# Loading and normalising the tokens of a decoder step: a diagonal matrix of the norm's factors in the transposing matmul, sample tokens first, and the first weight pair by feature blocks

## The chip, the cores and the metric

The kernel runs on one core of one Trainium2 chip. The core has a matrix engine (TensorE, PE in the profile; PEld is its loading of the stationary operand), three engines for elementwise work (VectorE = DVE, ScalarE = ACT, GpSimd = POOL) and SyncE (SP), from whose queue this kernel issues all its transfers. The metric is the time of one execution in microseconds, the median of several runs.

## The reference

One step of a one-layer decoder over 1,024 prompt tokens and 8 x 4 sample tokens, all in float32, model width 1,024, feed-forward width 2,816:

```python
def rmsnorm(x, g):
    y = xf * lax.rsqrt(jnp.mean(xf * xf, axis=-1, keepdims=True) + RMS_EPS)
    return (y * g.astype(jnp.float32)).astype(x.dtype)

def swiglu(x, w_gate, w_up, w_down):
    return (jax.nn.silu(x @ w_gate) * (x @ w_up)) @ w_down

# trunk_layer
x = half_ffn(x, 0, 0, 1)             # x + 0.5 * rmsnorm(swiglu(rmsnorm(x, g0), ...), g1)
h = rmsnorm(x, g[2])                 # then one input projection, mLSTM heads and
...                                  # sliding-window attention heads
x = x + rmsnorm(u @ w_out[l], g[3])  # one output projection
x = half_ffn(x, 1, 4, 5)
```

The outputs are the new tokens and the new states and caches. For the sample sequences the new key and value caches are the last 124 of the 128 old rows followed by the 4 new ones.

## The kernel before

**Layout.** The tokens are cut into four quarters q = 0..3. A quarter holds 256 prompt tokens and 8 sample tokens, so that its moving operand has 264 columns (`QW`). Features lie on the 128 partitions, in 8 blocks k = 0..7, kept in four tiles kp = 0..3 of two blocks each. Since tokens come from memory with a token on each partition, they are transposed on TensorE when they are loaded.

**Precision.** Each float32 operand of a large product is split into a high part (`Xh`, `wh`, a cast on ACT, L196) and the rest (`Xl`, `wl`, a subtraction on DVE, L197). A product is then three matmuls: high by high, high by low, low by high (`mm3` and the loops in `ffn`, all issued in `pe`, L154; transposes are issued there at L151).

**Loading (`load_tokens`, `token_norm`, `load_x`, L296 to L369).** For each quarter four transfers bring 128 x 512 pieces of the prompt (L298); for q = 0 two more bring the sample tokens after them. ACT and DVE sum the squares (L314, L317), and `rstd` makes the factor 1/root in ten small DVE instructions (L265 to L276), two of which make the first guess from the bits of the number. Meanwhile TensorE transposes the raw tokens in 16 transposes into four PSUM banks (`xT`, L151), ACT copies each bank out (`xr`, L353), POOL copies the sample columns in (L356). The factors are put on a row by six PE instructions (`rb`) and copied to `rrow` (L283). The raw tokens are stored in a scratch for the residual (`stash`, L290). `blocks` (L380) then multiplies each half tile by gain and row on DVE (`xb`, L385) and splits it (`Xh`, `Xl`). `sums` (L393) makes differences of these blocks, which the fast matrix products of the later weight pairs use.

**The feed-forward part (`ffn`, L694).** The 22 column blocks of the gate and up matrices are taken in 11 pairs. Pair p = 0 is multiplied plainly (`NPLAIN` = 1, tiles `pl`): for each quarter, each matrix and each column block m, the eight feature blocks are summed in one PSUM bank, 8 x 3 matmuls; 384 in all. From p = 1 on, a scheme with seven products in place of eight is used (tiles `gu`), on sums and differences made by `sums`. Then comes the down product (`pd`). Weights arrive as 512 KB transfers in two `raw` buffers (`plain_units`, `gu_units`, L634 and L670) and are split as units, four units ahead (`AHEAD` = 3).

**Order.** `Order` runs generators beside the matmul loops: each `yield` gives a delay in estimated PE time, `tick` runs what is due after each product, `need` runs tasks until a key is there, `take` hands out the next split weights. `XW` and `XQ` are the delays of loading. The framework then schedules the instructions of each engine in its own order from an estimate of when they are ready, within the data's dependencies; `high_priority` blocks go ahead. Each engine runs its list in order. After the program's start `load_x(0)` runs until the second tile is split, then weights are filled, then the other quarters are spawned (`program`, L1760).

**Later.** `post` (L428) ends each product that goes back to the residual: it loads the stored tokens (`x`, from `xs`), computes the norm of the product, adds, and stores. `swa_sample` (L1190) handles the sample's attention; it copies the 124 old cache rows from memory to memory with two transfers (L1195), and loads the old caches again as tiles `kc` and `vc`. `Last.finish` holds the end of the kernel: a `rstd`, then the last output tiles.

## Time and profile before

| what | value |
| --- | --- |
| median of 3 runs | 2020.64 us (2015.86 to 2020.72) |
| the profiled execution's own time | 2019.21 us |
| its span, first to last instruction | 2017.4 us |
| mean granted TensorE clock | 0.996 |
| PE busy | 1986.5 us, 16,178 matmul instructions |
| DVE busy | 1168.4 us |
| ACT busy | 874.9 us |
| POOL busy | 35.6 us |
| bytes moved, mean rate | 216.66 MB, 107 GB/s |

The span begins with the first instruction and ends with the last; the execution's own time is 1.81 us longer. Times in the views are microseconds from the span's start. A busy PE is not a PE at its best pace: matmuls overlap, so what counts is the distance from the start of one to the start of the next. A row of the timeline gives the start, the time from the first start to the last end, the engine, the line, the operation, the tiles (out<-in), the shapes, the number of instructions merged, and in brackets the idle time before it with what ended it. A row of a stage table gives the stretch, its length and the busy time of each engine with the number of instructions.

### The profile page before, as it was taken

To read this page: it belongs to the slowest core of one execution; us is meant where nothing else is said; L and a number is where in the kernel's file an instruction comes from. 1 tells how busy PE (TensorE), PEld (TensorE's weight loads), DVE (VectorE), ACT (ScalarE), POOL (GpSimd) and SP (SyncE) were. 2 spreads that over 40 slices of the span, in tenths; PEclk is the share of its full clock that TensorE was granted. 3 is DMA by queue.
4 is the path that set the end of the run, shared out by engine and by line. 5 is a ranking of instruction groups with operands and counts; after the bars stand their busy time and mean duration, and the time that the engine had idled before them with its cause. 6 is when DMAs were issued, how large, how long until landed. Compare 5 with 4: busy or idle time off the path is not lost.

```text
span 2017.4 us, 40347 instructions
## 1 busy us (share of the span) xinstructions
PE 1986.5 (98%) x16178; PEld 1942.6 (96%) x16178; DVE 1168.4 (58%) x2822; ACT 874.9 (43%) x2087; POOL 35.6 (2%) x166
## 2 busy tenths in 40 slices
PE   7999999999999999999999999999999999999997
PEld 7999999999999999987999999999999999999997
DVE  5855555557238436467556758785555556534764
ACT  6533333336336332346244655353333334533553
POOL 0000000000000001100101000000000000000000
PEclk9999999999999999999999999999999999999999
DMA  6122222226346343201214143322222223545773
GB/s 234 65 85 77 90 69 74 76 95 177 108 142 208 104 102 124 68 1 38 68 53 134 57 133 116 108 78 82 65 84 80 91 64 120 167 129 162 226 223 116
DMA packets 279690, 216.66 MB, mean 107 GB/s; under 512 B 21032, under 2 KB 252640, under 8 KB 279488
## 3 DMA queue, kind: packets, MB, share of 16 engines
q1 hardware_dynamic: 279504, 214.11, 35.0%
q8 instruction: 126, 2.06, 0.5%
q14 instruction: 60, 0.49, 0.1%
HBM read 172.39 MB, written 42.49 MB: 107 GB/s over the span
## 4 chain that ended last, share of the span: by engine, by line
PE 91%; DVE 3%; DMA 3%; ACT 2%; issue 1%; SPq 0%; DVEq 0%; ACTq 0%
PE gu L154 41%; PE pd L154 23%; PE pz L154 7%; PE pw L154 4%; PE pl L154 4%; PE pv L154 3%; PE po L154 2%; DMA raw<-ffn_w_down 2%; PE cs L154 1%; PE rb L154 1%; PE swo L154 1%; PE sws L154 1%; PE E L154 1%; ACT wh L196 1%; PE swp L151 1%
## 5 line engine op out<-in xcount | busy, mean ns | idle before, releaser
L154 PE MATMUL gu<-Xh,wh 128*128 128x264 f32 x2240 | 636.6, 284 | 0.0
L154 PE MATMUL gu<-Xl,wh 128*128 128x264 f32 x2240 | 636.0, 284 | 0.0
L154 PE MATMUL gu<-Xh,wl 128*128 128x264 f32 x2240 | 635.1, 284 | 0.0
L197 DVE TENSOR_TENSOR wl<-raw,wh 128x512 fp32r<-128x512 f32 x458 | 301.6, 670 | 384.3 <-ACT wh L196 376.5
L154 PE MATMUL pd<-hq,wh 128*128 128x264 f32 x2816 | 520.8, 286 | 0.1
L196 ACT CAST wh<-raw 128x512 fp32r<-128x512 f32 x458 | 270.1, 602 | 459.4 <-PE pd L154 193.2
L154 PEld LDWEIGHTS pd<-hq,wh 128*128 128x128 f32 x2816 | 437.8, 189 | 0.4 <-ACT yo L853 0.4
L154 PEld LDWEIGHTS gu<-Xh,wh 128*128 128x128 f32 x2240 | 421.1, 188 | 0.5 <-ACT sc L752 0.2
L154 PEld LDWEIGHTS gu<-Xh,wl 128*128 128x128 f32 x2240 | 421.6, 188 | 0.0
L154 PEld LDWEIGHTS gu<-Xl,wh 128*128 128x128 f32 x2240 | 421.3, 188 | 0.0
L154 PE MATMUL pd<-hq,wl 128*128 128x264 f32 x1408 | 401.1, 285 | 0.0
L154 PEld LDWEIGHTS pd<-hq,wl 128*128 128x128 f32 x1408 | 265.4, 188 | 0.2 <-DVE wl L197 0.2
L752 ACT COPY sc<-gu 128x264 f32<-128x264 f32 x240 | 91.0, 380 | 272.2 <-PE gu L154 268.0
L197 DVE TENSOR_TENSOR wl<-ws,wh 128x512 fp32r<-128x512 f32 x160 | 108.8, 690 | 87.6 <-ACT wh L196 84.7
L763 DVE TENSOR_TENSOR h<-gu,sc 128x264 f32<-128x264 f32 x120 | 51.8, 432 | 102.2 <-PE gu L154 83.3
L154 PE MATMUL pz<-xh,wh 128*128 128x264 f32 x352 | 102.3, 291 | 0.6 <-DVE z L1684 0.6
L154 PE MATMUL pz<-xh,wl 128*128 128x264 f32 x352 | 100.8, 286 | 0.0
L154 PE MATMUL pz<-xl,wh 128*128 128x264 f32 x352 | 100.5, 285 | 0.0
L196 ACT CAST wh<-ws 128x512 fp32r<-128x512 f32 x160 | 95.9, 623 | 4.1 <-PE pl L154 2.5
L764 ACT ACTIVATE h<-h 128x264 f32<-128x264 f32 x120 | 50.9, 425 | 106.5 <-DVE h L763 106.5
L769 DVE TENSOR_TENSOR sc<-gu,sc 128x264 f32<-128x264 f32 x120 | 51.6, 432 | 56.8 <-PE gu L154 51.4
L154 PE MATMUL pl<-Xh,wh 128*128 128x264 f32 x256 | 72.9, 299 | 3.3 <-ACT Xh L196 2.1
(368 smaller groups left out, 2969.6 us busy)
## 6 DMA issues: line engine op xcount, KB each, us to landing
raw<-ffn_w_down SPq DMA_DIRECT2D x80, 512.0 KB
raw<-ffn_w_gate SPq DMA_DIRECT2D x44, 512.0 KB
raw<-ffn_w_up SPq DMA_DIRECT2D x44, 512.0 KB
h<-h SPq DMA_DIRECT2D x80, 264.0 KB
hq<-h SPq DMA_DIRECT2D x160, 132.0 KB
raw<-ffn_w_down SPq DMA_DIRECT2D x40, 384.0 KB
x<-xs SPq DMA_DIRECT2D x48, 264.0 KB
raw<-w_in SPq DMA_DIRECT2D x21, 512.0 KB
```

The costliest lines, as they stand in the source:

```text
L151: K.nc.tensor.transpose(out, lhsT, rhs)
L154: K.nc.tensor.matmul(out, lhsT, rhs, start=start, stop=stop, **kw)
L196: K.nc.scalar.copy(hi, src)
L197: (eng or K.nc.vector).tensor_tensor(lo, src, hi.bitcast(F32), op=ALU.subtract)
L752: nc.scalar.copy(sc[n][:, g], ps)
L763: nc.vector.tensor_tensor(d, bk[tg, g], sc[n][:, g], op=ALU.add)
L764: nc.scalar.activation(d, d, AF.Silu)
L769: nc.vector.tensor_tensor(sc[n][:, g], src, sc[n][:, g], op=ALU.add)
```

## The change

The loading and the first pair are rewritten; smaller edits follow from that.

- Transfers: sample tokens first, then the four pieces of quarter 0, then the weights of pair 0 as eight 256 KB pieces, one for two feature blocks of one matrix (`first_loads`), then quarter 1 into the two `raw` buffers. The tables for the Silu function are asked for at the start (`warm`).
- The norm comes before the transposing: `token_norm` gives the factor r and its inverse. A diagonal matrix of r (`diagonal`, one DVE instruction for 128 tokens) is the moving operand of an ordinary float32 matmul (L154's form) in place of the identity in a transpose, so that the bank holds normalised tokens, transposed.
- Out of the bank ACT writes the high part with the gain as scale (two halves), DVE writes the low part in one instruction for each half, and ACT copies the normalised tokens to `xn`. `blocks` is no longer used there. POOL copies the sample columns into three tiles in place of one.
- The scratch for the residual now holds normalised tokens, and `post` of phase 1 multiplies them by the inverse factor (one DVE instruction for each of 16 tiles). `sums` of phase 0 has to multiply by the gain itself (for each pair of quarters 8 half tiles on DVE and 8 on ACT).
- `first_pair` multiplies quarter 0 feature tile by feature tile into four banks at a time; quarters 1 to 3 go column block by column block as before.
- `rstd` makes its first guess in one instruction in place of two, everywhere in the kernel.
- The memory-to-memory copies of the caches are gone; four transfers from `kc` and `vc` write those rows.

```diff
-XW = [2.0, 0.15, 0.2]
+XW = [2.0, 0.15, 4.0]
-XQ = [0, 0.0, 4.0, 10.0]
+XQ = [0, 3.0, 10.0, 20.0]
-SUMS = {(2, 0, 0): 0, (3, 0, 0): 1}
+SUMS = {1: {(1, 1, 1): 0, (3, 0, 0): 1}, 3: {(2, 0, 0): 0, (3, 0, 0): 1}}
...
+    K.C, K.vs = [K.cp.tile([P, 4, 129], F32, tag=x, name=x) for x in ("C", "vs")]
...
+def gain_rows(K):
...
+    return graw
+def load_gains(K, graw):
...
+def rstd(K, ss, scale=1.0 / D, eps=EPS, root=False):
     nc.vector.tensor_scalar(v, ss, scale, eps, op0=ALU.mult, op1=ALU.add)
-    ri = r.bitcast(I32)
-    nc.vector.tensor_scalar(ri, v.bitcast(I32), 1, None, op0=ALU.arith_shift_right)
-    nc.vector.tensor_scalar(ri, ri, -1.0, float(0x5F3759DF), op0=ALU.mult, op1=ALU.add)
+    nc.vector.tensor_scalar(r.bitcast(I32), v.bitcast(I32), -0.5, float(0x5F3759DF), op0=ALU.mult, op1=ALU.add)
     nc.vector.tensor_tensor(t, r, v, op=ALU.mult)
     nc.vector.tensor_tensor(t, t, r, op=ALU.mult)
...
     nc.vector.scalar_tensor_tensor(t, r, -0.5 * 0.375 ** 3, v, op0=ALU.mult, op1=ALU.mult)
     nc.vector.tensor_tensor(t, t, r, op=ALU.mult)
     nc.vector.scalar_tensor_tensor(r, t, 1.5 * 0.375, r, op0=ALU.add, op1=ALU.mult)
...
+    nc.vector.tensor_tensor(u, v, r, op=ALU.mult)
+    return r, u
...
+def load_tokens(K, q):
+    if q == 1:
+        t = [raw_tile(K, [2, 512]) for _ in range(2)]
+        K.t[q] = [[x[:, i] for i in range(2)] for x in t]
+    else:
+        K.t[q] = [[slot(K, "xt")[:, 0:512] for _ in range(2)] for _ in range(2)]
     for i in range(2):
...
+        for j in range(2):
+            K.nc.sync.dma_start(K.t[q][j][i],
+                                K.A["x_prompt"][0, (2 * q + j) * P:(2 * q + j + 1) * P, i * 512:(i + 1) * 512])
+def first_loads(K):
+    A, nc = K.A, K.nc
+    K.t, K.w0 = {}, {}
+    K.xt = [slot(K, "xt")[0:32, 0:512] for _ in range(2)]
+    for i in range(2):
+        nc.sync.dma_start(K.xt[i], A["x_sample"].rearrange("b t d -> (b t) d")[:, i * 512:(i + 1) * 512])
+    load_tokens(K, 0)
+    for kp in range(4):
+        for mat, n in enumerate(("ffn_w_gate", "ffn_w_up")):
+            K.w0[kp, mat] = slot(K, "w0")[:, 0:512].rearrange("p (k m) -> p k m", k=2)
+            nc.sync.dma_start(K.w0[kp, mat], A[n][0, 0].rearrange("(k p) m -> p k m", p=P)[:, 2 * kp:2 * kp + 2, 0:256])
+    load_tokens(K, 1)
 def token_norm(K, tt, both=False):
...
-    for j, t in enumerate(tt):
+    for j, t in reversed([*enumerate(tt)]):
         for i in range(2):
             o = ss[0:w, n * i + j:n * i + j + 1]
-            if both and i == 0:
+            if both and (w < P or (j == 0 and i)):
                 nc.vector.tensor_tensor_reduce(out=jk, in0=t[i], in1=t[i], scale=1.0, scalar=0.0,
                                                op0=ALU.mult, op1=ALU.add, accum_out=o)
             else:
                 nc.scalar.activation(jk, t[i], AF.Square, accum_out=o)
     s = small(K, "xsn", n)
     nc.vector.tensor_tensor(s, ss[:, 0:n], ss[:, n:2 * n], op=ALU.add)
-    return rstd(K, s)
+    return rstd(K, s, root=True)
+def diagonal(K, r, w, i):
+    d = K.C[0:w, i, 0:w]
+    K.last = K.nc.vector.tensor_scalar(d, K.ident[0:w, 0:w], r, None, op0=ALU.mult).ins
+    return d
 def load_sample(K):
...
+    r, ri = token_norm(K, [K.xt], True)
+    K.xtr = K.cp.tile([32, 1], F32, tag="xtr", name="xtr")
+    nc.vector.tensor_copy(K.xtr, ri[0:32])
+    d = diagonal(K, r[0:32], 32, 2)
+    ps = sbank(K, "xsT")
     for k in range(KT):
...
+        pe(K, ps[:, 32 * k:32 * k + 32], K.xt[k // 4][:, (k % 4) * P:(k % 4) * P + P], d)
+    yield
+    a, x = K.vs.rearrange("p h v -> p (h v)"), slot(K, "xsg", F32R)
+    xn, g, hi, lo = [t[:, o:o + 256].rearrange("p (k t) -> p k t", k=KT) for t, o in ((a, 0), (a, 256), (x, 0), (x, 256))]
+    nc.vector.tensor_copy(xn, ps[:, 0:256].rearrange("p (k t) -> p k t", k=KT))
+    nc.vector.tensor_tensor(g, xn, K.gain[:, 0:KT].unsqueeze(2).to_broadcast([P, KT, 32]), op=ALU.mult)
+    split(K, g, hi, lo)
+    K.xs0 = xn, hi, lo
 def load_x(K, q):
...
+    tt = K.t[q]
     if q == 0:
...
+        K.low, dec = [], load_sample(K)
+        next(dec)
+    r, ri = token_norm(K, tt, q == 0)
+    dg = [diagonal(K, r[:, j:j + 1], P, 2 * (q % 2) + j) for j in range(2)]
+    if q == 0:
+        K.low.append(K.last)
+        with K.tc.issue_after(K.last):
+            next(dec, None)
+    K.X[q], xn = [], []
     for kp in range(4):
         ps = bank(K, "xT")
         for i in range(2):
             k = 2 * kp + i
             for j, t in enumerate(tt):
-                pe(K, ps[:, (2 * i + j) * P:(2 * i + j + 1) * P], t[k // 4][:, (k % 4) * P:(k % 4) * P + P], K.ident,
-                   tr=True)
-        nc.scalar.copy(pair(x[kp])[:, :, 0:2 * P], ps.rearrange("p (a t) -> p a t", a=2))
...
-        nc.gpsimd.tensor_copy(pair(x[kp])[:, :, 2 * P:QW], K.xsT[:, 2 * kp:2 * kp + 2, 8 * q:8 * q + 8])
+                pe(K, ps[:, (2 * i + j) * P:(2 * i + j + 1) * P], t[k // 4][:, (k % 4) * P:(k % 4) * P + P], dg[j])
+        hi, lo, x = slot(K, "Xh", F32R), slot(K, "Xl", F32R), slot(K, "xn")
+        h2, l2, x2 = pair(hi), pair(lo), pair(x)
+        for i in range(2):
+            nc.scalar.activation(h2[:, i, 0:2 * P], ps[:, i * 2 * P:(i + 1) * 2 * P], AF.Copy,
+                                 scale=K.gain[:, 2 * kp + i:2 * kp + i + 1])
+        for i in range(2):
+            ins = nc.vector.scalar_tensor_tensor(l2[:, i, 0:2 * P], ps[:, i * 2 * P:(i + 1) * 2 * P],
+                                                 K.gain[:, 2 * kp + i:2 * kp + i + 1], h2[:, i, 0:2 * P].bitcast(F32),
+                                                 op0=ALU.mult, op1=ALU.subtract)
+        if q == 0:
+            K.low.append(ins.ins)
+        nc.scalar.copy(x2[:, :, 0:2 * P], ps.rearrange("p (a t) -> p a t", a=2))
+        for d, a in zip((x2, h2, l2), K.xs0):
+            nc.gpsimd.tensor_copy(d[:, :, 2 * P:QW], a[:, 2 * kp:2 * kp + 2, 8 * q:8 * q + 8])
+        xn.append(x)
+        K.X[q].append((h2, l2))
+        K.od.done.add(("b", 0, q, kp))
         yield XW[1]
...
+    if q < 2:
+        load_tokens(K, q + 2)
+    yield XW[2]
+    ps = sbank(K, "rb")
+    for j in range(2):
+        pe(K, ps[:, j * P:(j + 1) * P], ri[:, j:j + 1].to_broadcast([P, P]), K.ident)
+    pe(K, ps[:, 2 * P:QW], K.xtr.to_broadcast([32, P]), K.ident[0:32, 8 * q:8 * q + 8])
+    set_row(K, q, ps[:, 0:QW])
     for kp in range(4):
...
-    yield from blocks(K, 0, q, x, 0)
+        stash(K, q, kp, xn[kp])
+    K.b[q] = xn
+    K.od.done.add(("B", q))
...
+    if phase == 0:
+        for kp in (2, 0, 1, 3):
+            for q in (2 * g + 1, 2 * g):
+                b = slot(K, "xb")
+                for i in range(2):
+                    s, gk = slice(i * QW, (i + 1) * QW), K.gain[:, 2 * kp + i:2 * kp + i + 1]
+                    if q % 2:
+                        nc.vector.tensor_scalar(b[:, s], K.b[q][kp][:, s], gk, None, op0=ALU.mult)
+                    else:
+                        nc.scalar.activation(b[:, s], K.b[q][kp][:, s], AF.Copy, scale=gk)
+                K.b[q][kp] = b
+            yield NP[0]
...
+    K.od.done.add(("S", phase, g))
...
+        if phase == 1:
+            nc.vector.tensor_tensor(pair(t), pair(t), K.r[q].unsqueeze(1).to_broadcast([P, 2, QW]), op=ALU.mult)
...
+def first_units(K):
+    def part(kp, mat):
+        with K.tc.issue_after(K.low[kp]):
+            return wsplit(K, K.w0[kp, mat])
+    return [lambda kp=kp, mat=mat: part(kp, mat) for kp in range(4) for mat in range(2)]
 def ffn_units(K, j):
     for p in range(MT // 2):
+        if j == 0 and p == 0:
+            yield from first_units(K)
+            continue
             yield from (plain_units if p < NPLAIN else gu_units)(K, w, p)
...
+def first_pair(K, sg):
+    nc, od = K.nc, K.od
+    ws = {}
+    def mm(ps, kp, mat, m, x, i):
+        k = 2 * kp + i
+        xh, xl = [t[:, i] for t in x[kp]]
+        wh, wl = [w[:, i, m * P:(m + 1) * P] for w in ws[kp, mat]]
+        pe(K, ps, wh, xh, start=(k == 0), stop=False)
+        pe(K, ps, wh, xl, start=False, stop=False)
+        pe(K, ps, wl, xh, start=False, stop=(k == KT - 1))
+        od.tick()
+    ps = {}
+    for m in range(2):
+        sg[m, 0] = slot(K, "h")
+        nc.gpsimd.memset(sg[m, 0][:, 0:1], 0.0)
+    for kp in range(4):
+        od.need(("b", 0, 0, kp))
+        for mat in range(2):
+            ws[kp, mat] = od.take()
+            for m in range(2):
+                if kp == 0:
+                    ps[mat, m] = bank(K, "pl", "ab"[mat])[:, 0:QW]
+                for i in range(2):
+                    mm(ps[mat, m], kp, mat, m, K.X[0], i)
+    for mat in range(2):
+        for m in range(2):
+            d = sg[m, 0][:, 0:QW]
+            if mat == 0:
+                nc.scalar.activation(d, ps[mat, m], AF.Silu)
+            else:
+                nc.vector.tensor_tensor(d, d, ps[mat, m], op=ALU.mult)
+    for q in range(1, NQ):
+        g, s = q // 2, slice((q % 2) * QW, (q % 2) * QW + QW)
+        for mat in range(2):
+            for m in range(2):
+                if (m, g) not in sg:
+                    sg[m, g] = slot(K, "h")
+                pq = bank(K, "pl", "ab"[mat])[:, 0:QW]
+                for kp in range(4):
+                    od.need(("b", 0, q, kp))
+                    for i in range(2):
+                        mm(pq, kp, mat, m, K.X[q], i)
+                g0 = SUMS[1].get((q, mat, m))
+                if g0 is not None:
+                    od.need(("B", 2 * g0), ("B", 2 * g0 + 1))
+                    od.spawn(sums(K, 0, g0))
+                d = sg[m, g][:, s]
+                if mat == 0:
+                    nc.scalar.activation(d, pq, AF.Silu)
+                else:
+                    nc.vector.tensor_tensor(d, d, pq, op=ALU.mult)
...
+        if p == 0 and phase == 1:
+            first_pair(K, sg)
+            for (m, g), t in sg.items():
+                hs[m, g] = store_h(K, m, g, t)
+            continue
...
+                    od.need(("S", phase - 1, g))
...
-    for nme, src in (("s_swa_k", "cache_swa_k"), ("s_swa_v", "cache_swa_v")):
-        nc.sync.dma_start(O[nme][0, :, 0:124].rearrange("b w v d -> b w (v d)"),
-                          A[src][0, :, 4:128].rearrange("b w v d -> b w (v d)"))
...
+        for nme, t in (("s_swa_k", kc), ("s_swa_v", vc)):
+            nc.sync.dma_start(O[nme][0, 4 * hf:4 * hf + 4, 0:124].rearrange("b w v d -> w b (v d)"),
+                              t[4:128].rearrange("p (b f) -> p b f", b=4))
...
-    load_gains(K)
+    warm = small(K, "warm", 1)
+    K.nc.scalar.activation(warm, K.ones, AF.Silu)
+    graw = gain_rows(K)
+    first_loads(K)
+    load_gains(K, graw)
-    K.od.need(("b", 0, 0, 1))
+    K.od.need(("b", 0, 0, 3))
     K.od.fill()
     for q in range(1, NQ):
         K.od.spawn(load_x(K, q), XQ[q])
```

More of the change, by code (lines that the diff above doesn't have):

```diff
@@ L276, in rstd @@
     nc.vector.scalar_tensor_tensor(r, t, 1.5 * 0.375, r, op0=ALU.add, op1=ALU.mult)
-    return r
+    if not root:
+        return r
+    nc.vector.tensor_tensor(u, v, r, op=ALU.mult)
+    return r, u
 def set_row(K, q, ps):
@@ L360, in load_x @@
-    with K.tc.high_priority():
-        ps = sbank(K, "rb")
-        for j in range(2):
-            pe(K, ps[:, j * P:(j + 1) * P], r[:, j:j + 1].to_broadcast([P, P]), K.ident)
-        pe(K, ps[:, 2 * P:QW], K.xtr.to_broadcast([32, P]), K.ident[0:32, 8 * q:8 * q + 8])
-        set_row(K, q, ps[:, 0:QW])
+                pe(K, ps[:, (2 * i + j) * P:(2 * i + j + 1) * P], t[k // 4][:, (k % 4) * P:(k % 4) * P + P], dg[j])
+        hi, lo, x = slot(K, "Xh", F32R), slot(K, "Xl", F32R), slot(K, "xn")
@@ L715, in ffn @@
                             od.tick()
-                        if p == 0 and (q, mat, m) in SUMS:
-                            od.spawn(sums(K, phase - 1, SUMS[q, mat, m]))
+                        if p == 0 and (q, mat, m) in SUMS[phase]:
+                            od.spawn(sums(K, phase - 1, SUMS[phase][q, mat, m]))
                         d = sg[m, g][:, s]
```

29 lines of the change are left out of this document (2 added, 27 removed).

## The prediction

> **What bounds the kernel now.** I read the page first, then a table by stages of the head, then the timeline of the first 40 us, then the chain of waits for the tail.
>
> ```profile
> span 2017.4 us, 40347 instructions
> PE 1986.5 (98%) x16178; PEld 1942.6 (96%) x16178; DVE 1168.4 (58%) x2822; ACT 874.9 (43%) x2087; POOL 35.6 (2%) x166
> PE 91%; DVE 3%; DMA 3%; ACT 2%; issue 1%; SPq 0%; DVEq 0%; ACTq 0%
> ```
>
> TensorE is busy for 98% of the span and makes 91% of the chain that ended last. So an instruction added on PE after the head costs its full distance, and a microsecond saved on DVE or ACT pays only where PE waits. The change works where PE is not yet full:
>
> ```profile
> 0.00:10.00 10.00, 3.27 (x16) 2.38 (x17) 2.90 (x17) 3.93 (x8) 0.74 (x7) 1.00 0.66 209
> 20.00:30.00 10.00, 8.28 (x52) 7.05 (x51) 4.78 (x17) 6.49 (x16) 0.00 (x0) 1.00 0.94 343
> 30.00:40.00 10.00, 10.00 (x81) 9.76 (x81) 6.46 (x20) 8.50 (x19) 0.00 (x0) 1.00 0.73 243
> ```
>
> The columns are stretch, length, busy PE, PEld, DVE, ACT, POOL, granted clock, DMA share and GB/s. From 30 us on PE is full. What can be won lies ahead of that; the timeline shows it:
>
> ```profile
> 8.77 0.63 ACT L317 ACTIVATE jk<-xt 32x512 f32<-32x512 f32 x1
> 9.31 0.18 ACT L317 ACTIVATION_READ_ACCUMULATOR jk<-xt 32x1 f32 x1
> ...
> 17.01 0.81 PE L154 MATMUL pl<-Xh,wh 128*128 128x264 f32 x2 [1.75 <-ACT Xh L196]
> ...
> 20.60 0.42 PE L154 MATMUL pl<-Xl,wh 128*128 128x264 f32 x1
> 20.82 0.42 PE L154 MATMUL pl<-Xh,wl 128*128 128x264 f32 x1
> ...
> 23.12 0.62 ACT L196 CAST wh<-raw 128x512 fp32r<-128x512 f32 x1 [3.91 <-DMA raw<-ffn_w_up]
> ...
> 23.79 0.39 PE L154 MATMUL pl<-Xh,wh 128*128 128x264 f32 x1 [1.11 <-ACT wh L196]
> ```
>
> The last of the six first loads has landed by 8.77, its square is summed at 9.49, and the first product of the feed-forward part starts at 17.01. Its matmuls then start 0.22 us apart, though the stage table says a granted clock of 1.00 there. Then PE waits for the up weights (23.12, 23.79). The first of the seven-product matmuls, which the change leaves alone, closes the head:
>
> ```profile
> 78.66 0.28 PE L154 MATMUL gu<-Xh,wh 128*128 128x264 f32 x1
> ```
>
> I measure the change by where this moment goes.
>
> **What a PE instruction costs.** Distances between starts, warm:
>
> ```profile
> 78.82 31.28 PE gu L154 x256
> ```
> ```profile
> 37.33 1.47 PE L151 MATMUL xT<-ident,xt 128*128 128x128 f32 x12
> ...
> 38.56 0.37 PE L154 MATMUL pl<-Xh,wh 128*128 128x264 f32 x1
> ```
> ```profile
> 1022.29 1.16 PE L154 MATMUL S<-z,z 128*128 128x128 f32 x8
> 1023.21 0.37 PE L154 MATMUL po<-xh,wh 128*128 128x264 f32 x1
> ```
> ```profile
> 31.02 0.71 PE L154 MATMUL rb<-ident,r 128*128 128x128 f32 x4
> ...
> 31.96 0.39 PE L154 MATMUL pl<-Xl,wh 128*128 128x264 f32 x1
> ```
>
> A 264-column matmul: 31.28 / 256 = 0.122 us. A transpose: (38.56 - 37.33) / 12 = 0.103. An ordinary float32 product of 128 x 128 x 128 is two instructions: `S` is such a product, its eight instructions take 1023.21 - 1022.29 = 0.92, so 0.115 each and 0.23 a product. The six instructions of `rb` take 31.96 - 31.02 = 0.94.
>
> **Where the head's time goes now.** From 17.01 to 78.66 are 61.65 us:
>
> ```profile
> 17.00:22.39 5.39, 5.38 (x23) 5.10 (x24) 2.86 (x6) 1.11 (x2) 0.00 (x0) 1.00 0.78 263
> 22.39:28.35 5.96, 4.24 (x29) 3.16 (x28) 3.16 (x12) 4.84 (x12) 0.00 (x0) 1.00 1.08 403
> ```
>
> 384 `pl` matmuls by 0.122 are 46.9, 48 transposes of quarters 1 to 3 by 0.103 are 4.9, three `rb` are 2.8: 54.6. The other 7.1 are losses. In the first stretch 23 matmuls took 5.39 where 2.8 was due: 2.6 lost to the slow pace. In the second 29 instructions, 16 of them transposes, took 5.96 where 3.2 was due: 2.7 lost, mostly to weights that came late. 1.8 lie elsewhere.
>
> **The change, part by part.**
>
> *Start of the transposing.* The norm now stands ahead of it. The same bytes are asked for first, in another order, so the last of them again lands at 8.77 and its square is summed at 9.49. Then come an addition and the nine small instructions left in `rstd`. Their price is in the chain at the kernel's end:
>
> ```profile
> 2008.54 0.17 DVE v L265
> ...
> 2010.52 2.07 DVE yo L606 x3
> ```
>
> Ten of them in 1.98 us. So r is there at 11.47. A diagonal is a 128 x 128 DVE instruction the trace does not have; the nearest rows are
>
> ```profile
> L919 DVE CAST identb<-ident 128x128 bf16<-128x128 f32 x1 | 0.2, 209 | 0.0
> L1506 DVE TENSOR_SCALAR snum<-snum,r 128x128 f32<-128x128 f32 x1 | 0.3, 281 | 0.0
> ```
>
> 0.21 to 0.28; I take 0.28, the same operation, and 0.15 for the handover: the first transposing product starts at 11.9. Bounds: 11.4 if the sample tokens, which went last, had held up the last landing; 12.7 if ACT squares the last piece and then another one (0.63 + 0.18 more).
>
> *Transposing of quarter 0.* 16 products, 32 instructions. PE has idled, so they run at the slow pace, which I put at 2 x 0.115 = 0.23 (`pl` shows 0.22 for 0.122). The slow pace lasted 5.4 us of `pl`; in 5.4 us go 23 instructions, the other 9 take 1.0: 6.4 in all, against 3.7 if the pace were full and 7.4 if it stayed slow. PE has work throughout, since three banks can be filled while ACT and DVE empty the first.
>
> [...]
>
> *The products.* 384 by 0.122 = 46.9, as before; the order by feature tiles adds none. Weights for all of them are asked for at the start: until the last has landed 3.3 MB must come, at 209 GB/s (the first 10 us) by about 18 us, at 343 by 12. Quarter 0's last tile wants them after 24 us. So the 2.7 us of waiting go, and what is late next is the next quarter.
>
> *Transposing of quarters 1 to 3.* 96 instructions by 0.115 = 11.0 in place of 4.9: 6.1 more, on a PE that has no idle time there. Nothing hides them. The four `rb` are 3.8; quarter 0's stood ahead of 17.01 and now stands behind the start.
>
> *What feeds PE.* From 11.9 to the end of quarter 0 PE needs 6.4 + 96 x 0.122 = 18.1 us. DVE must do in that time, by the rows
>
> ```profile
> L385 DVE SCALAR_TENSOR_TENSOR xb<-xr,gain,rrow 128x264 f32<-128x264 f32 x32 | 14.6, 487 | 1.8 <-ACT rrow L283 1.8
> L197 DVE TENSOR_TENSOR Xl<-xb,Xh 128x528 fp32r<-128x528 f32 x16 | 11.3, 706 | 6.3 <-ACT Xh L196 6.2
> L197 DVE TENSOR_TENSOR wl<-raw,wh 128x512 fp32r<-128x512 f32 x10 | 6.9, 690 | 4.5 <-ACT wh L196 4.4
> ...
> L353 ACT COPY xr<-xT 128x512 f32<-128x512 f32 x16 | 8.9, 592 | 0.8 <-PE xT L151 0.7
> ...
> L356 POOL COPY xr<-xsT 128x16 f32<-128x16 f32 x16 | 3.3, 260 | 9.6 <-DVE rt L271 9.6
> ```
>
> 8 `wl` (5.5), 8 low halves (3.9 at 0.487), three half tiles for the sample (1.5), quarter 1's norm and diagonals (12 x 0.2 + 2 x 0.28 = 3.0): 13.9. ACT: 8 casts of weights at 0.62, 4 x 2 high halves and 4 copies, at most 0.6 each (L353's, twice a half's size), 4 squares at 0.81: 15.4. Both fit with 4.2 and 2.7 to spare; if that cover goes, PE waits for the excess. In place of the old waits I take 2.0 for all that remains: the 1.8 that lay elsewhere and 0.2 for the new handovers. POOL's 32 further copies of 16 columns (0.26 each) and the `memset` are beside this.
>
> *The other edits.* The table load for Silu, the two memory-to-memory copies of the caches that leave SP's queue in the head, and the transfers that take their place later cost nothing that PE waits for now; were the four later ones (1 MB) uncovered, at 343 GB/s they would cost 3 us. `post` of phase 1 gets 16 DVE instructions like `Xl`'s, 11.3 us. There,
>
> ```profile
> 625.00:650.00 25.00, 23.45 (x182) 23.24 (x181) 20.20 (x52) 13.91 (x30) 0.00 (x0) 0.93 0.50 166
> ```
>
> DVE is busy for 20.2 of 25, so 5.6 of them (two quarters) just do not fit beside it; PE is not held, since its weights are split four units ahead. I price it at nothing, with 3 as the upper bound. `rstd` is one instruction shorter: 0.2 off the tail, and 0.2 off the one wait of PE for it below.
>
> **Sum.** 11.9 + 6.4 + 46.9 + 11.0 + 3.8 + 2.0 = 82.0 in place of 78.66: 3.3 later. Less 0.4: 2.9 us. The profiled execution took 2019.21 us; it lies between the lowest (2015.86) and the median (2020.64) of the three runs, and close to their mean of 2019.07. I add to it: **2022 us**.
>
> **Rivals.**
>
> *The pace falls back (slower).* PE's idle time has a price of its own elsewhere:
>
> ```profile
> 632.81 1.16 PE L154 MATMUL rb<-ident,r 128*128 128x128 f32 x6 [1.55 <-DVE v L265]
> ...
> 634.41 0.42 PE L154 MATMUL pd<-hq,wl 128*128 128x264 f32 x1
> 634.63 0.64 PE L154 MATMUL pd<-hq,wh 128*128 128x264 f32 x2
> ```
>
> After 1.55 us idle the matmuls are 0.22 apart; after the wait that ended at 23.79 (1.11) they were not. If PE's list puts the first products ahead of the second tile's transposes, PE runs dry at 11.9 + 8 x 0.23 + 0.3 = 14.0 and waits for two high halves (1.2) and a copy of sample columns (0.26): 1.5 us, right at that point. Each such stop costs 1.5 and then 2.6 of slow pace, 4.1 in all. One gives 2026, two (again at the second feature tile) give 2030. For it: DVE and ACT alternate within every tile. Against: three free banks.
>
> *The price without the return.* [...] As a mechanism of this kernel: the 6.1 us are paid and the 2.7 us of waiting stay, because quarter 1, whose loads now stand behind all the weights, is late in the place of the weights: 2022 + 2.7 = 2024.8. For it: ACT has 2.7 us to spare by a bound, no more. Against: the loads of quarter 1 left SP's queue behind waits before, and now do not.
>
> *A head without losses.* [...] The head cannot give 0.3%, 6.1 us: PE's own work from 11.4 on, 46.9 + 3.7 + 11.0 + 3.8, ends at 76.8.
>
> **How the numbers follow.** Forecast 0.57; the pace falling back 0.15; price without return 0.14; no losses 0.14. Over 0.3%, which is about what a measurement of this kernel can tell from no change, means below 2014.6 or above 2026.7. No case reaches the first by itself; the scatter of the runs (4.9 us) leaves 0.05 for it. Two stops, or one with DVE in `post` uncovered, reach the second, with the scatter: 0.16. The rest, 0.79, is no change. The range takes in the case without losses less a little scatter and the case of two stops: 2015.5 to 2030.
>
> **What would show it.** In the changed profile: `xT` as 128 instructions in L154's form, 0.115 apart when warm, the first at 11.9; the first `pl` between 14 and 18; pace 0.12 from about 17.5; no wait for a weights transfer; the first `gu` at 82; ten steps of `rstd` become nine. It would be wrong if the first `gu` came before 77 or after 87, or if the difference lay behind the head: in the waits of `rb` around 630 and 765, or in the mixing part where the cache rows are now written.

## The result, and the profile after

The changed kernel takes 2034.49 us (median of 4 runs, 2032.21 to 2036.58); the kernel before takes 2018.41 in 4 runs. The ratio is 1.0084, with a 95% interval of 1.0063 to 1.0105: slower by some 16 us, above the upper end of the range (2030). The head, on which nearly all of the working went, came out as forecast. What was missed lies behind it.

The page of the changed kernel, the lines that answer to those of before:

```profile
span 2034.8 us, 40604 instructions
PE 2001.9 (98%) x16250; PEld 1958.4 (96%) x16250; DVE 1173.8 (58%) x2832; ACT 881.4 (43%) x2120; POOL 43.7 (2%) x200
PE 87%; DMA 5%; DVE 4%; ACT 2%; issue 1%; SPq 0%; DVEq 0%; ACTq 0%
```

PE is busy for 98% again, and its part of the chain that ended last has gone down from 91% to 87%: waits that were beside the path have come onto it. The stage table of the head and its timeline:

```profile
0.00:10.00 10.00, 2.54 (x12) 2.40 (x12) 4.47 (x28) 3.59 (x9) 0.70 (x6) 1.00 0.67 198
20.00:30.00 10.00, 10.00 (x85) 9.84 (x84) 4.95 (x20) 4.05 (x12) 4.56 (x26) 1.00 0.60 188
30.00:40.00 10.00, 9.55 (x79) 9.22 (x78) 5.94 (x21) 8.26 (x23) 0.00 (x0) 1.00 0.67 213
```
```profile
9.24 0.61 ACT L347 ACTIVATE jk<-xt 128x512 f32<-128x512 f32 x1
9.76 0.18 ACT L347 ACTIVATION_READ_ACCUMULATOR jk<-xt 128x1 f32 x1
...
12.37 5.40 PE L160 MATMUL xT<-C,xt 128*128 128x128 f32 x24 [0.97 <-DMA w<-ffn_w_up]
...
17.61 0.39 PE L160 MATMUL rb<-ident,ru 128*128 128x128 f32 x2
...
17.75 0.73 PE L160 MATMUL pl<-Xh,wh 128*128 128x264 f32 x4
```
```profile
28.30 2.84 PE L160 MATMUL xT<-C,raw 128*128 128x128 f32 x24
...
30.98 0.39 PE L160 MATMUL rb<-ident,ru 128*128 128x128 f32 x2
```
```profile
81.96 0.28 PE L160 MATMUL gu<-Xh,wh 128*128 128x264 f32 x1
```

Between 20 and 30 us PE is full where it had gaps before; between 30 and 40 us it now has 0.45 us of them. The first 24 instructions of the transposing products take 17.61 - 12.37 = 5.24 us, 0.22 each; warm ones take (30.98 - 28.30) / 24 = 0.11. The first `gu` starts at 81.96; 82.0 was forecast.

So the loss has to be sought later. The table gives the time between the first matmuls of successive tiles, read from PE's rows in two traces of each kernel (the unchanged kernels were run once more, below as e1 and e5):

| stage | before | changed | difference of the means |
| --- | --- | --- | --- |
| start to first `gu` | 78.66, 79.14 | 81.96, 81.57 | +2.9 |
| `gu` of the first feed-forward part | 408.70, 408.69 | 411.17, 410.82 | +2.3 |
| `pd` | 266.63, 265.19 | 265.28, 266.75 | +0.1 |
| `pz` to `pv` (input projection) | 66.05, 66.07 | 68.16, 68.72 | +2.4 |
| `pv` to `n0T` | 272.58, 272.58 | 273.41, 273.42 | +0.8 |
| `n0T` to `snT` (states of the sample sequences) | 22.80, 22.68 | 29.42, 29.43 | +6.7 |
| `snT` to `gu` of the second part | 192.04, 192.05 | 191.48, 189.97 | -1.3 |
| `gu` of the second part | 418.14, 417.93 | 420.62, 420.99 | +2.8 |
| its `pd` to the end | 291.78, 290.10 | 293.27, 288.73 | +0.1 |
| span | 2017.38, 2014.43 | 2034.77, 2030.40 | +16.7 |

Four rows behind the head carry 14.2 of the 16.7: `pz`, the states, and the two stages of `gu`; the change alters no matmul in any of them. The experiments take them one by one.

### The profile page after: what moved, and what is told of

The parts are those of the page before. It is cut to its first block, busy times and chain, and to the rows that moved or that the text cites. A ratio compares the mean times of both kernels' runs of the same rounds, so it can differ in the third digit from the quotient of the medians.

```text
span 2034.8 us, 40604 instructions
## 1 busy us (share of the span) xinstructions
PE 2001.9 (98%) x16250; PEld 1958.4 (96%) x16250; DVE 1173.8 (58%) x2832; ACT 881.4 (43%) x2120; POOL 43.7 (2%) x200
## 4 chain that ended last, share of the span: by engine, by line
PE 87%; DMA 5%; DVE 4%; ACT 2%; issue 1%; SPq 0%; DVEq 0%; ACTq 0%
PE gu L160 40%; PE pd L160 20%; PE pz L160 6%; PE pw L160 5%; PE pl L160 4%; DMA raw<-ffn_w_down 3%; PE pv L160 3%; PE po L160 2%; DVE wl L203 1%; PE cs L160 1%; PE swo L160 1%; PE sws L160 1%; ACT wh L202 1%; PE rb L160 1%; PE xT L160 1%
## 5 line engine op out<-in xcount | busy, mean ns | idle before, releaser
L203 DVE TENSOR_TENSOR wl<-raw,wh 128x512 fp32r<-128x512 f32 x450 | 296.1, 669 | 383.1 <-ACT wh L202 377.5
L202 ACT CAST wh<-raw 128x512 fp32r<-128x512 f32 x450 | 265.0, 601 | 453.2 <-PE pd L160 194.2
L160 PE MATMUL pw<-uh,wh 128*128 128x264 f32 x256 | 73.9, 289 | 0.0
```

The costliest lines, as they stand in the source:

```text
L160: K.nc.tensor.matmul(out, lhsT, rhs, start=start, stop=stop, **kw)
L202: K.nc.scalar.copy(hi, src)
L203: (eng or K.nc.vector).tensor_tensor(lo, src, hi.bitcast(F32), op=ALU.subtract)
```

## The experiments

Ratios are to the kernel before, run beside each on the same chip; in brackets the 95% interval.

**The two kernels again (e1, e5).** No edit.

> The kernel before, unchanged, for a second trace of it. The head of the changed kernel ended where it was forecast (first gu at 82.0 us); 14 us more are lost behind it. Theory A (the loss behind the head hangs on PE waits that stand at the edge of the slow pace, so that it comes and goes from run to run): this trace shows the wait ahead of the sample's states (sinter) or those of the later stages differing by over 0.5 us from the first trace, stage lengths scattering by 2 us or more, ratio 1.000 within 0.003. Theory B (an edit of the change costs it steadily): stages repeat within 1 us.

> The changed kernel once more, for a second trace. Per-program theory: the steady length of a weight pair (40.89 us in the first feed-forward part, 41.07 in the second, against 40.80 and 40.83 before) and PE's wait of 1.9 us around 780 for the eviction of a projection bank repeat to 0.05 and 0.2 us. Chance theory: they differ. The 6.6 us at the sample's states (slow pace from 1113 to 1127) I expect to come and go: with them the execution takes about 2036, without about 2031.

Measured: 2018.16 us, 0.9999 [0.9988, 1.0011], and 2034.68 us, 1.0085 [1.0068, 1.0101]. The second columns of the table come from these two traces. In the changed kernel the stages that grew repeat to 0.6 us; the one of the states, whose loss had been expected to come and go, repeats to 0.01. `pd` and the last stage differ by up to 4.5 us between two traces of one kernel, so nothing is read from them.

**The products taken out (e2), and put in alone (e8).** In e2 the changed kernel transposes with the identity, which leaves out the norm's factors of the prompt tokens; in e8 the kernel before gets ordinary products with the identity.

```diff
-                pe(K, ps[...], t[...][...], dg[j])                 # e2
+                pe(K, ps[...], t[...][...], K.ident, tr=True)
...
-                pe(K, ps[...], t[...][...], K.ident, tr=True)      # e8
+                pe(K, ps[...], t[...][...], K.ident)
```

> The changed kernel with the 64 transposing products of the prompt done as transposes by the identity again; it leaves out the norm's factor on the prompt's tokens in the first feed-forward part, all else stays. If PE is full from the start of quarter 0's transposing on, 128 instructions of 0.115 give way to 64 of 0.103: 8.1 us less in the head at the full pace, first gu near 74, and up to 3 us less again or more by the slow pace of quarter 0; the time falls from 2034.5 to 2026. If waits for DVE and ACT take the place of the products (rival), the first gu falls by 3 us or less.

> The kernel before with its 64 transposes of prompt tokens done as ordinary float32 products with the identity. Quarters 1 to 3: 96 instructions of 0.115 for 48 of 0.103, 6.1 us more on a PE without idle time from 30 us on; quarter 0's are done while the norm is under way, so at most 2 us more there. If ordinary products bring up PE's pace and transposes don't, the first pl matmuls are 0.12 apart and not 0.22, 2.6 us less. So the first gu at 78.66 + 6.1 + 0 to 2 - 2.6 = 82 to 84 with that rule, 85 to 87 without; the time 2022 or 2025.

Measured: e2 2024.03 us, 1.003 [1.002, 1.0041], first `gu` at 73.61, that is 8.35 ahead of the changed kernel; e8 2023.67 us, 1.0028 [1.0019, 1.0038], first `gu` at 84.26. Alone the products cost 5.6 us, with the first `gu` just above the 82 to 84 that was expected if they bring up PE's pace. In e8 they are the ones that run at the slow pace, and the first `pl` behind them do not:

```profile
14.57 3.64 PE L154 MATMUL xT<-ident,xt 128*128 128x128 f32 x16
...
20.52 0.29 PE L154 MATMUL pl<-Xh,wh 128*128 128x264 f32 x1
20.64 0.28 PE L154 MATMUL pl<-Xl,wh 128*128 128x264 f32 x1
20.76 0.28 PE L154 MATMUL pl<-Xh,wl 128*128 128x264 f32 x1
```

Sixteen in 3.64 us are 0.23 each, the `pl` are 0.12 apart. In the kernel before, with transposes in their place, 23 `pl` took 5.39 us first. In the trace of before PE had nothing but transposes, without a gap, from 8.43 to 12.03 us, and the pace came up only at 22.16; in e8 it had nothing but products from 14.57 to 18.21, and `pl` are 0.12 apart from 20.39 on. e2 took 10.4 us off and not 8.35; in its trace the stage of the states takes 24.17 us in place of 29.42, so the products have a share in that loss as well.

**The small edits of the rest (e3, e4).** e3 is the changed kernel with the memory-to-memory cache copies and the longer `rstd` of before; e4 is the kernel before with the new ones.

```diff
-    nc.vector.tensor_scalar(r.bitcast(I32), v.bitcast(I32), -0.5, float(0x5F3759DF), ...)      # e3; e4 the other way
+    nc.vector.tensor_scalar(ri, v.bitcast(I32), 1, None, op0=ALU.arith_shift_right)
+    nc.vector.tensor_scalar(ri, ri, -1.0, float(0x5F3759DF), op0=ALU.mult, op1=ALU.add)
...
+        nc.sync.dma_start(O[nme][0, :, 0:124]..., A[src][0, :, 4:128]...)
-            nc.sync.dma_start(O[nme][0, 4 * hf:4 * hf + 4, 0:124]..., t[4:128]...)
```

> The changed kernel with two edits undone: the caches' 124 rows are copied from memory to memory again, and rstd makes its first guess in two instructions. Theory B: one of these costs the 14 us behind the head, so the time falls to 2021 to 2026. Theory A: within 3 us of the changed kernel, 2031 to 2037.

> The kernel before with those two edits made alone. Theory B: 2026 to 2032 in place of 2018. Theory A: 2015 to 2021.

Measured: e3 2033.96 us, 1.0091 [1.0063, 1.012]; e4 2019.94 us, 1.0017 [1.0007, 1.0026]. So these edits do not carry the loss. Alone they cost 1.4 to 5.2 us by the interval (1.9 between the medians) where -0.4 was forecast; the trace of e4 shows no single place for it. The trace of e3 is that of its slowest execution (2042.75 us) and has its first `gu` at 89.21. The copies are asked for at 19.05 and 42.90 there, at 16.31 and 20.42 in the kernel before; whether they hold that head up is not shown, so e3 does not price them.

**The multiplication in `post` (e6, e7).** e6 takes the 16 instructions out of the changed kernel (the residual then stays normalised); e7 puts 16 of the same size, by ones, into the kernel before.

```diff
-            nc.vector.tensor_tensor(pair(t), pair(t), K.r[q].unsqueeze(1)..., op=ALU.mult)   # e6
...
+            nc.vector.tensor_tensor(pair(t), pair(t), K.ones.unsqueeze(1)..., op=ALU.mult)   # e7
```

> The changed kernel without the multiplication by the inverse factor in post of phase 1: the residual then takes the normalised tokens, which is not the reference's sum; all else stays. If these 16 DVE instructions hold up the eviction for which PE waits 1.9 us at 780, the wait goes and the time falls by 2 to 4 us, to 2031. Rival (they lie beside PE's work, as forecast): no change, 2033 to 2036.

> The kernel before with 16 multiplications of the same shape and place in post of phase 1, by ones: if they hold up the eviction, a wait of about 1.9 us comes up around 775 and the time rises by 2 us, to 2020; rival: no wait, 2018.

Measured: e6 2025.89 us, 1.0038 [1.0023, 1.0053]; e7 2021.62 us, 1.0019 [1.0006, 1.0031]. The view of waits, PE's only, 600 to 1000 us (engine, line and tile, what ended the wait, us in total, times, longest), for before, changed, and e7:

```profile
PE rb L154 <- DVE v L265: 1.5, 1, 1.5
PE pz L154 <- DVE z L1684: 0.6, 1, 0.6
```
```profile
PE pz L160 <- DVE z L1839: 2.3, 2, 1.9
...
PE cs L160 <- DVE sq L250: 1.3, 2, 1.0
```
```profile
PE pz L154 <- DVE z L1686: 2.7, 2, 1.9
...
PE cs L154 <- DVE sq L244: 1.5, 1, 1.5
```

The wait of `pz` for the eviction `z` grows from 0.6 to 2.3 and 2.7, and in e6 it is not in the list; the stage from `pz` to `pv` takes 65.56 us in e6 and 68.65 in e7. The timeline of the changed kernel shows how, VectorE's list first and then PE's:

```profile
773.57 0.70 DVE L515 TENSOR_TENSOR x<-x,rrow 128x528 f32<-128x528 f32 x1
...
778.09 0.49 DVE L546 SCALAR_TENSOR_TENSOR xl<-y,gain,xh 128x264 fp32r<-128x264 f32 x1
778.49 0.70 DVE L537 TENSOR_TENSOR sq<-sq,sq 128x528 f32<-128x528 f32 x1
779.11 0.49 DVE L546 SCALAR_TENSOR_TENSOR xl<-y,gain,xh 128x264 fp32r<-128x264 f32 x1
779.51 0.43 DVE L1839 SCALAR_TENSOR_TENSOR z<-pz,rrow 128x264 f32<-128x264 f32 x1
```
```profile
777.85 0.28 PE L160 MATMUL pz<-xh,wl 128*128 128x264 f32 x1
779.99 0.39 PE L160 MATMUL pz<-xh,wh 128*128 128x264 f32 x1 [1.86 <-DVE z L1839]
```

The bank is full at 778, its eviction is behind three instructions of `post` in VectorE's list, and TensorE has no free bank until 779.99. L515 is the new multiplication; VectorE had no idle time from 773 to 781, so its 0.70 us moved all that stood behind it.

**The multiplication on GpSimd (e14).** The changed kernel with the states six ahead (e9, below) and the 16 instructions on the idle engine.

```diff
-            nc.vector.tensor_tensor(pair(t), pair(t), K.r[q].unsqueeze(1)..., op=ALU.mult)
+            nc.gpsimd.tensor_tensor(pair(t), pair(t), K.r[q].unsqueeze(1)..., op=ALU.mult)
```

> The changed kernel with the states six ahead, and with the 16 multiplications of `post` in the first phase put on GpSimd instead of VectorE. Theory A (PE's wait of 1.9 us before `pz` at about 780 comes from VectorE's queue, where the eviction of `pz` stands behind the work of `post`): that wait goes or falls below 0.6, the stage from `pz` to `pv` goes from 70.4 to 66 to 67, and the time to 2022 to 2024. [...]

Measured: 2033.72 us, 1.0079 [1.006, 1.0098], against 2026.1 for e9. The waits of PE, 600 to 1000 us:

```profile
PE cs L160 <- DVE sq L250: 2.9, 2, 2.5
PE rb L160 <- DVE r L281: 2.6, 2, 2.5
...
PE pz L160 <- DVE z L1839: 0.9, 1, 0.9
```

Theory A holds a part, but had neither the time nor the stage (71.41 us). With the queue relieved, the wait of `pz` falls to 0.9; with 1.3 to 1.8 us on GpSimd for each tile (below, two of the timeline's rows) in place of 0.70, the chain of `post` gets longer, and PE waits for the norm's sums and factors instead. On either engine the multiplication makes PE wait.

```profile
768.13 1.81 POOL L515 TENSOR_TENSOR x<-x,rrow 128x528 f32<-128x528 f32 x1 [127.43 <-DMA x<-xs]
...
771.31 1.32 POOL L515 TENSOR_TENSOR x<-x,rrow 128x528 f32<-128x528 f32 x1
```

**The states of the sample sequences (e9).** The next state is asked for two steps earlier.

```diff
-    for b in range(4):
+    for b in range(6):
         state(b)
...
-        for b in range(len(states), min(b0 + 4, 8)):
+        for b in range(len(states), min(b0 + 6, 8)):
```

> The changed kernel with the sample's states loaded six ahead instead of four, so that the transfer of the next states is asked for two steps of work earlier. Theory A (the 6.6 us of the states' stage come from PE's wait of 1.4 us for `Cb<-state_mlstm_C`, after which it runs at the slow pace): the wait at about 1113 goes, the products behind it stay 0.12 apart, the stage from `n0T` to `snT` goes back from 29.4 to 23 to 24, and the time is about 2028 to 2029. Theory B (the slow pace there comes from the low share of matmuls in this stage, whatever the wait): the stage stays at 28 to 30 and the time within 2 us of 2034.5.

Measured: 2026.1 us, 1.0047 [1.0033, 1.0061]; the stage takes 21.04 us in place of 29.42. PE's row in the kernel before, its rows in the changed kernel, then the stage tables of the changed kernel and of e9 (PE, granted clock, DMA share, GB/s):

```profile
1104.68 0.43 PE L154 MATMUL sinter<-Cb,qm 128*32 128x129 f32 x8 [0.64 <-DMA Cb<-state_mlstm_C]
```
```profile
1112.78 0.43 PE L160 MATMUL sinter<-Cb,qm 128*32 128x129 f32 x8 [1.39 <-DMA Cb<-state_mlstm_C]
...
1115.12 0.59 PE L160 MATMUL po<-xh,wh 128*128 128x264 f32 x1
1115.51 0.42 PE L160 MATMUL po<-xl,wh 128*128 128x264 f32 x1
1115.73 0.42 PE L160 MATMUL po<-xh,wl 128*128 128x264 f32 x1
```
```profile
1112.00:1116.00 4.00, 3.22 (x26) 0.65 0.92 261
1116.00:1120.00 4.00, 4.00 (x23) 0.50 0.45 131
1120.00:1124.00 4.00, 4.00 (x31) 0.50 0.45 131
1124.00:1128.00 4.00, 4.00 (x22) 0.64 0.44 131
```
```profile
1112.00:1116.00 4.00, 4.00 (x51) 1.00 1.02 290
1116.00:1120.00 4.00, 4.00 (x52) 1.00 0.68 199
```

The wait for `Cb` is 1.39 us (0.64 in the kernel before), and behind it the granted clock is 0.50 for more than 8 us: `po` is 0.22 apart. In e9 that wait is gone, the clock is 1.00 throughout, and the stage is even shorter than before. Theory A is right, and the gain is larger than it said (23 to 24 us). That the wait alone is enough for the half clock is refuted by e16, below.

**One buffer further on (e12, e16).** One buffer of the rotating pool, from which weights, tokens and states take their tiles, is taken ahead of everything, in the kernel before (e12) and in the changed one (e16). In both, every engine's list stays the same instruction for instruction, but for the one `memset`.

```diff
+    nc.vector.memset(slot(K, "unused"), 0.0)
     load_gains(K)                                # e12; in e16 ahead of first_loads
```

> The kernel before with one buffer of the rotating pool of 2112 bytes a partition taken, and set to zero, ahead of everything else, so that all later tiles of that pool (weights, tokens, sums) sit one buffer further on; nothing else is changed. Theory A (the steady pace of the pairs of gate and up tiles depends on which buffers the operands of TensorE and of the other engines share): the pairs no longer take 40.80 and 40.83 us, in at least one of the two parts by over 0.03, with up to 3 us in the whole time. Theory B (it depends on the order of the instructions alone): 40.80 and 40.83 within 0.03, and 2016 to 2019 us.

> The changed kernel with one buffer of the rotating pool taken and set to zero ahead of everything else; every engine's list of instructions stays as it is but for that one memset. Theory A (the steady pace of the pairs comes from which buffers are used): the pairs' 40.89 and 41.07 us change by over 0.03 in at least one part. Theory B (the order alone): 40.89 and 41.07 again. For the sample's states: if the late second load and the slow stretch come from the order of work, the stage from `n0T` to `snT` is 29.4 again, and if they come from the buffers, it is 23 to 25.

Measured: e12 2020.96 us, 1.0011 [0.9999, 1.0023]; e16 2031.25 us, 1.0076 [1.0056, 1.0096]. In e16 the states' stage takes 23.53 us, although the wait is there:

```profile
1115.86 0.43 PE L160 MATMUL sinter<-Cb,qm 128*32 128x129 f32 x8 [1.38 <-DMA Cb<-state_mlstm_C]
...
1117.47 0.39 PE L160 MATMUL po<-xh,wh 128*128 128x264 f32 x1
1117.70 0.29 PE L160 MATMUL po<-xl,wh 128*128 128x264 f32 x1
1117.82 0.28 PE L160 MATMUL po<-xh,wl 128*128 128x264 f32 x1
```

The same list of work and the same wait, and no half clock. e6 has a wait of 1.47 us there, and no half clock either. So the late load alone does not bring the half clock.

The five long waits of `sinter`, and the granted clock behind each:

| trace | wait, us | clock behind it |
| --- | --- | --- |
| changed | 1.39 | 0.50 for 13.65 us |
| e5 | 1.36 | 0.50 for 13.65 us |
| e3 | 1.68 | 0.50 for 13.65 us |
| e6 | 1.47 | 1.00 |
| e16 | 1.38 | 1.00 |

The length of the wait does not tell the two kinds apart: 1.36 and 1.39 us have the half clock behind them, 1.38 and 1.47 do not. Nor does it for the waits of some 0.5 us: e11 has 0.52 and no fall, e2 0.53 and half the clock for 3.41 us. What decides is not shown, and so it is open whether every execution of the changed kernel has the 6.7 us that both of its traces have.

What stays open is why the second load is late: the first product that needs it starts 3.9 us after the load is asked for in the changed kernel (also in e5), 3.1 in the kernel before (also in e1). In e16 it is 3.9 too, so the buffers are not it. The long wait stands in the five traces above, and neither in those without the products (e2, e11), nor with the states asked for six ahead (e9, e14), nor in those made from the kernel before.

To the other buffers the steady pace does answer. The stage tables of `gu` alone, before, changed, e12 (stretch, length, PE busy with the number of matmuls, clock, DMA share, GB/s):

```profile
250.00:450.00 200.00, 200.00 (x1650) 1.00 0.25 78
1500.00:1700.00 200.00, 200.00 (x1648) 1.00 0.27 85
```
```profile
250.00:450.00 200.00, 200.00 (x1645) 1.00 0.25 77
1500.00:1700.00 200.00, 200.00 (x1639) 1.00 0.24 75
```
```profile
250.00:450.00 200.00, 200.00 (x1644) 1.00 0.25 77
1500.00:1700.00 200.00, 200.00 (x1650) 1.00 0.27 85
```

In 200 us of a full PE at full clock the changed kernel makes 5 and 9 matmuls fewer. By the starts, a pair of 336 matmuls takes 40.80 and 40.83 us before (the same in e1), 40.89 and 41.07 changed (the same in e5), 40.93 and 40.79 in e12, 40.92 and 40.92 in e16. Theory A: which buffers are used moves the pace. The shift does not bring the changed kernel back to 40.80 and 40.83, so that its own loss of pace comes from its buffers is likely and not shown. Ten pairs in each part make 0.9 and 2.4 us of the loss in the two `gu` stages; of the rest of the first, 0.8 is in its first pair (41.77 us in place of 40.98), whose sums come late.

**All tiles 128 bytes further on (e10).** The kernel before with an unused tile ahead of the constants.

```diff
+    K.pad = K.cp.tile([P, 32], F32, tag="pad", name="pad")
+    nc.vector.memset(K.pad, 0.0)
```

> The kernel before with one unused tile of 128 bytes a partition ahead of its other constants, so that every later tile lies 128 bytes further on in SBUF; one memset of it is added. Theory A (the small steady differences between programs, 40.80 to 41.07 us a pair of gate and up tiles, come from where the tiles lie in SBUF): the pairs of the two feed-forward parts no longer take 40.80 and 40.83 us but something else between 40.7 and 41.1, and the time moves by up to 4 us either way. Theory B (they come from the order of the instructions): the pairs take 40.80 and 40.83 again, within 0.03, and the time is that of the kernel before, 2018, within 1.5 us.

Measured: 2018.31 us, 1.0003 [0.9992, 1.0014], 40.80 and 40.83 us a pair. A common shift of 128 bytes does nothing; with e12, it is which buffer serves which tile that counts, not where the pool begins by so little. What in the buffers does it is not settled.

**Both parts out (e11).** The changed kernel with the edits of e2 and e6 together.

> The changed kernel with two things out: the tokens are transposed with the identity again (so the norm's factors of the prompt tokens are left out) and the residual isn't multiplied back in `post`. Each alone took 10.4 and 8.6 us off the 2034.5. Theory A (both removed the same 5 to 6 us of slow pace at the sample's states, so the two overlap): the head ends at about 73.6, no wait before `pz`, the states' stage is at 23 to 24, and the time is 2019 to 2022, that is 13 to 15 us off. Theory B (the two are independent): 19 us off, 2015 to 2016.

Measured: 2018.66 us, 1.0009 [0.9999, 1.0018], first `gu` at 75.75 (there the first 18 `pl` went at the slow pace), no wait ahead of `pz`, the states' stage at 22.69. In ratios e2 took off 0.0055, e6 0.0047, both together 0.0076: they overlap by 0.0026 or 5 us. The intervals alone would not carry this; the traces do. At the states e2 takes off 5.3 us, e6 5.8, both together 6.7: e2 shortens the wait to 0.52 us, and in e6 a wait of 1.47 us happened not to bring the half clock. Theory A, though the first `gu` comes 2 us later than the 73.6 it had. What is left of the change, its loads, order and small edits, wins 3 us in the head and gives it back later.

**Versions without the two costs (e13, v1, v2, v3).** e13 is the kernel before with the edit of e9. v1 is the kernel before with the change's loads, feature-block order and cache writes, without its products and multiplications; v2 and v3 also hold the splits of the weights behind quarter 0's work on ScalarE and VectorE, v2 the later quarters' squares too, and both have e9's edit.

```diff
+    def part(kp, mat):                                                                          # v2, v3
+        with K.tc.issue_after(K.low[kp]), K.tc.issue_after(K.hi[1 + max(0, kp - 1)]):
+            return wsplit(K, K.w0[kp, mat])
```

> The kernel before with the sample's states loaded six ahead instead of four. Theory A (the wait for `Cb<-state_mlstm_C`, 0.54 to 0.64 us here, is all that is to be had): the stage from `n0T` to `snT` goes from 22.7 to 21 to 22.2 us, and the time to 2015.5 to 2017.5 beside a kernel before at 2017 to 2018, 0.9990 to 0.9998. Rival (the slots that two more states hold are taken from weights, which then come late): the stages around it get longer by 1 us or more and the time is 2018 to 2021.

> The kernel before with the change's order of loads (all of the first pair's weights asked for at the start, as eight pieces), its feature-block order of the first pair and its later cache writes, but with transposes as transposes, the norm's factors applied in the blocks and the residual left as the raw tokens, so no multiplication in `post`. Theory (what the change's loads save in the head is the 2.7 us of waiting for weights, and only the diagonal products and the multiplications cost): first `gu` at 74 to 77 instead of 78.7 to 79.1, no wait before `pz`, and 2014 to 2017, 0.998 to 0.9995 of the kernel before. Rival (the norm's factors, which come later than the transposes, now hold the blocks back, or a later stage gives the gain back): first `gu` at 78 or later, or 2018 to 2021.

> The kernel before with the first loads and feature-block order of the trial of loads and order, but with each weight's split held behind the first quarter's own work on ScalarE and VectorE, the next quarters' squares too, and the states loaded six ahead. Theory (that trial lost 4.5 us ahead of its first `pl`, at 21.4 instead of 16.9, because four weight casts stood ahead of the copies of quarter 0 on ScalarE, and won 4.3 behind it): first `pl` at 16.5 to 18, first `gu` at 74 to 76.5, and 2012 to 2016 us, 0.9975 to 0.9992 of the kernel before. Rival (quarter 1 then comes late for the same reason, so that the wait only moves): first `gu` at 78 to 80, and 2016 to 2020.

> The trial with held weights, with the holds taken off from the third quarter on (there the first sums had gone ahead of quarter 3's blocks on VectorE, and PE waited 5.6 us at 69.8). Theory: first `pl` at 17 to 18.5, no wait over 1.5 us in the head, first `gu` at 75 to 77, and 2013 to 2016.5 us, 0.998 to 0.9995 of the kernel before. Rival (the head stays at 79 or more, since what feeds quarter 1 is late): 2016 to 2020.

Measured: e13 2015.97 us, 0.9991 [0.9982, 1.0], stage 21.03; v1 2021.35 us, 1.0023 [1.0013, 1.0033], first `pl` at 21.40, first `gu` at 79.33; v2 2022.51 us, 1.0026 [1.0016, 1.0035], first `gu` at 83.01; v3 2018.58 us, 1.0002 [0.9993, 1.0011], first `gu` at 78.74. PE's waits in the heads of v1 and v3:

```profile
21.40 0.59 PE L159 MATMUL pl<-Xh,wh 128*128 128x264 f32 x1 [2.87 <-ACT Xh L201]
```
```profile
37.47 0.51 PE L159 MATMUL pl<-Xh,wh 128*128 128x264 f32 x2 [3.05 <-ACT Xh L201]
```

The weights' wait of 2.7 us goes in all three, and each time another one of 2.9 to 5.6 us (v2, at 69.8, for quarter 3) takes its place, for the same two engines. Early weights pay nothing here, since ScalarE and VectorE must split them at the moment when the tokens need these engines. The rivals were right for v1, v2 and v3 in kind (v2 is slower than its rival said, and the head of v3 ends just ahead of it), theory A for e13. e13 is the lowest of all versions, by 0.1% against the kernel before, with an interval that just reaches 1.

## Why the prediction was wrong, step by step

- **Start of the transposing.** Within its bounds in the first trace, 12.37 (11.9 forecast, 11.4 to 12.7), and just outside them in e5, 12.93. The last square is summed at 9.94 instead of 9.49.
- **Quarter 0.** Right in the first trace, 24 instructions at the slow pace in 5.24 us (23 in 5.4 forecast), the rest warm, with work for PE throughout; the close hit is luck: the clock rises 5.18 us after the first product in this trace, but 2.90 us after it in e5. There the later start and the shorter slow stretch make up for each other.
- **Products, quarters 1 to 3, remainder.** Right: 0.112 for a warm instruction (0.115), longest wait in the first pair 0.45 us, first `gu` at 81.96 and 81.57 (82.0). Of the rivals for the head none happened. The case without losses, which sets the lower end of the range, needs a pace that is full from the start of the transposing, and no run shows that: it was slow for 5.18 us here and for 2.90 in e5. Ordinary products cost more than transposes here: e8, which changes nothing else, loses 5.6 us, and e2 wins 10.4.
- **The other edits at nothing, -0.4 for `rstd`.** Wrong: e4 costs 1.4 to 5.2 us, which neither fits -0.4 nor tells whether the bound of 3 us for the cache rows held.
- **The step that failed: "PE is not held, since its weights are split four units ahead. I price it at nothing, with 3 as the upper bound."** It looked at the weights' queue and not at the other thing that VectorE owes to PE, the eviction of `pz`. That wait costs the stage 2.4 us (e7 alone: 2.6), near the upper bound and not nothing.
- **What no step had:** the half clock at the states (6.7 us), which stands behind a load that comes late (waits of 1.39 and 1.36 us), though not behind each such wait (1.38 in e16), and a steady pace (3.3 us) of the kind that changes with the buffers. Behind the head the sum had -0.4 us and the traces show 13.8 more; these two make 10.0 of it. Both sit in work whose matmuls the change does not touch. Removing the multiplications took 8.6 us off, but 5.8 of them at the states, 330 us later; in e16 the states lose nothing to the clock with the multiplications in place, so that part is no price of theirs.

The prediction had named the mixing part and the waits of VectorE as the places where it would be wrong; it gave them too little weight. The rival of the falling pace had the right mechanism, an idle PE and then 0.22 us between matmuls, and the wrong place.

## What to carry to other kernels

Where a change adds work to an engine, list all that this engine owes to the busiest one, evictions of PSUM banks among them, and not only the queue that was tuned last. Where a trace shows the matrix engine waiting for a load in a stage of small products, count what half the clock would cost there (here 6.7 us behind waits of 1.39 and 1.36), and load earlier: two lines did that here (e9, e13). Where two kernels differ by some 0.1% in a steady loop whose code is the same, shift one buffer before explaining it.

## What the runs showed of the hardware

- A full TensorE at granted clock 1.00 kept paces of 40.79 (e12) to 41.07 us (changed) for the same 336 matmuls in these programs, steady to 0.01 from the fifth pair on within one program and in its repetition (e1, e5); with every engine's list unchanged, one buffer's rotation moved it by 0.13 and -0.04 us (e12).
- The views show a granted clock of 1.00 in the head while `pl` or the products ran at 0.22 us, and 0.50 at the states with the same 0.22. The record of the clock in these traces begins only where the slow pace ends (22.16 us before, 17.55 changed), so the 1.00 ahead of it rests on no record. There the distance between starts is the only sign.
- From there to 2012.1 us before and 2028.0 changed, the record has 0.50 at 633.14 for 3.41 us and at 1288.50 for 6.83 us in the kernel before, and at 1113.23 for 13.65, at 1304.37 for 3.41 and at 1952.91 for 3.41 us in the changed one, and 1.00 elsewhere.
- A wait of 1.36 to 1.68 us at the states was followed by the half clock in three traces (changed, e5, e3), and waits of 1.38 and 1.47 us were not in two others (e16, e6); waits of 0.5 to 0.6 us were followed by 3.41 us of it in some traces (e2, e7, e8, e10, e12) and by none in others (before, e1, e4, e11, v1).
- The same multiplication of 128 x 528 float32 takes 0.70 us on VectorE and 1.3 to 1.8 on GpSimd.
